# The emitter's price for a transpose on TensorE: one pass of the array in place of two, and the instruction order that follows

## The chip, the cores and the metric

The kernel runs on one core of one Trainium2 chip. The metric is the device time of one execution in microseconds (us). The profile is one execution seen by the hardware profiler; its span runs from the first to the last instruction. The engines are PE (TensorE, matmuls; PEld is its weight load), DVE (VectorE), ACT (ScalarE), POOL (GpSimd) and SP (the queue that issues every DMA). Each engine works through its own list of instructions in order, and an instruction that waits holds up all that stand behind it on that engine.

## The reference

Two layers over 2048 latent tokens of width 1024 with a context prefix of 256 tokens. Both layers are modulated by a conditioning vector ("ada"), normalised by RMS, gated by SiLU and added to the stream; a last RMSNorm ends the program.

```python
# layer 0 (even): windowed attention with context and sink, beside a bidirectional S5 state space
q, k, v, g_attn, u, g_ssm = jnp.split(a @ w_in, cuts, axis=-1)
o_attn = window_attention(q, k, v, kc, vc, sink) * jax.nn.silu(g_attn)
o_ssm, o_ssm_c = s5_branch(u, uc, ...)            # scans in both directions, GELU, GLU with a 512x512 matrix
y = jnp.concatenate([o_attn, o_ssm * jax.nn.silu(g_ssm)], axis=-1) @ w_out
# layer 1 (odd): pooling over 2, 4, 8 and 16 neighbours in four channel groups
u, gate = jnp.split(a @ w_in, 2, axis=-1)
p = jnp.einsum('btgc,gcd->btgd', multiscale_pool(u), pool_w) * pool_scale
y = (p * jax.nn.silu(gate)) @ w_out
```

Attention has 8 query heads on 2 key heads, blocks of 128 queries, each against three blocks of keys and the 256 context keys.

## The kernel before, in words

All data lie transposed (channels on the 128 partitions, tokens along the row). Large matrix products run in a 32-bit format of one pass, with operands split into a high and a low part: three matmuls of 128x128 by 512 columns make one product step (`products`, `mm`), eight steps a tile. Small products stay in plain f32.

**Who sets the order.** The kernel is written as some 35 generators, one for each stream of work (`t_main` for the input products, then the output product `t_out0` and the second layer; `t_ltab` and `t_lags` for the S5 lag kernels; `t_etab` for rotation tables; `t_gen`, `t_s5`, `t_rot`, `t_s5out` for the scan; `t_kv`, `t_qk`, `t_exp`, `t_norm`, `t_pv` for attention; `t_glu`, `t_fold`, `t_mix` beside it). While the program is built, an emitter (class `Threads`) keeps a clock for each engine. Every instruction is charged a duration (`use`, which calls `issue`): it starts at the latest of its engine's clock, its inputs and the readers of what it overwrites, and moves that clock. The stream that would be ready first by these clocks is continued next, and what it emits goes to the end of the engines' lists. The PE's charge passes through `array`, which doubles it while the emitter takes the array for slow. So a charge changes no instruction; it changes which stream comes next, and with it the place of instructions on all engines.

**What else looks at the clocks.** `lighter(n)` puts an elementwise operation on DVE or on POOL, whichever clock would be done first (with POOL's charge doubled); the splits, the rotation tables, the lag tables, the scan's rotations and others go through it. So a changed clock also moves operations between these two engines.

**Turns.** A turn is a 128x128 transpose: a matmul against the identity (`transpose`, line 508). There are 848: 624 in `t_pv`, 128 in `t_s5`, 48 in `t_kv` and 48 of two columns in the two ada streams.

**The stages, in the order of the span.** 0 to 50 us: modulation of layer 0. 50 to 260: norm, the `u` products, rotation and lag tables. 260 to 735: the other input products, with the S5 scan between them until 654. 735 to 1168: attention in 32 units (one key head and one block of 128 queries) and 156 items (one unit and one block of keys). For an item, `t_pv` issues four turns of probabilities into one of two PSUM banks, ACT copies the high part, DVE subtracts for the low part, and two matmuls follow; the turns of item j+1 stand ahead of the matmuls of item j. Beside it run `t_fold` (until 884 us) and `t_glu` (809 to 954 us); from 1032 us on the output product `t_out0` runs beside it. 1168 to the end: the rest of the output product and layer 1, matmul behind matmul.

`t_out0` needs the weight space that `t_glu` gives back at its end, and the mixed activations (`t_mixin`, `t_mix`) of a quarter of the tokens.

Of the kernel before, what the change touches and what calls it, by code (L numbers as in the profile page):

```python
# [289 lines left out]
def body(ctx: ExitStack, tc: tile.TileContext, I, out):  # L290
    nc = tc.nc
    V, G, S, TE = nc.vector, nc.gpsimd, nc.scalar, nc.tensor
# [166 lines left out]
    def use(e, c, outs, *ins, port=False):  # L459
        th.issue(ename[id(e)], c, outs, [x for x in ins if isinstance(x, bass.AP)], port)  # L460
# [43 lines left out]
        return TE.matmul(o, w, x, start=start, stop=stop)  # L504

    def transpose(o, i, ident):
        use(TE, 0.22, [o], i)
        return TE.transpose(o, i, ident)  # L508

    def dma(o, i):  # L510
# [66 lines left out]
    def t_ada0():  # L577
# [22 lines left out]
        for i in range(KT):  # L600
            g, half = divmod(i, 2)
            yield from arrived(w[i])
            t_ = shaped(w.pop(i), (4, 512))
            ps = bank(g % 2)[0:2]
            for k in range(4):
                mm(ps, s2.f[:, 4 * half + k], t_[:, k], i % 2 == k == 0, half == 1 and k == 3)
            yield
            load(i + NADA)
            if i == 1:
                flags.add("ada_l1")  # L610
            if half == 1:
                r = row.next()[0:2]
                act(r, ps, AF.Copy, scale=0.5)
                yield
                for j in range(4):
                    transpose(bank(2)[:, 8 * g + 2 * j:8 * g + 2 * j + 2], r[:, 128 * j:128 * (j + 1)], K["ident"][0:2, 0:2])
                yield
                sl = slice(2 * g, 2 * g + 2)
                for r, sh, gs in ((1, shc, gsc), (0, sh0, gs0)):
                    tt(V, sh[:, sl], got[:, 0, r, g], K["b0"][:, sl], OP.add)  # L620
                    tt(V, gs[:, sl], got[:, 1, r, g], K["b0"][:, 8:16][:, sl], OP.add)
                    stt(gs[:, sl], gs[:, sl], 1.0, K["g0"][:, sl], OP.add, OP.mult)
                flags.add(f"ada0{g}")
                yield
# [5 lines left out]
    def t_ada1():  # L630
# [13 lines left out]
        for blk in range(8):  # L644
            b = yield from get_bank()
            ps = bank(b)
            for i in range(4):
                yield from arrived(w[4 * blk + i])
                t_ = w.pop(4 * blk + i)
                for k in range(2):  # L650
                    mm(ps[0:2], silu.f[:, 2 * i + k], t_[:, k], i == k == 0, i == 3 and k == 1)
                yield
                load(4 * blk + i + NADA1)
            r = row.f[0:2]
            act(r, ps[0:2], AF.Copy, scale=0.5)
            yield
            for j in range(4):
                transpose(ps[:, 2 * j:2 * j + 2], r[:, 128 * j:128 * (j + 1)], K["ident"][0:2, 0:2])
            yield
            got = ps[:, 0:8:2]  # L660
            vec, sl = (gate0, sh1, gs1, gate1)[blk // 2], slice(4 * (blk % 2), 4 * (blk % 2) + 4)
            add = (K["b0"][:, 16:24], K["b1"][:, 0:8], K["b1"][:, 8:16], K["b1"][:, 16:24])[blk // 2]
            tt(V, vec[:, sl], got, add[:, sl], OP.add)
            put_bank(b)
            if blk // 2 == 2:
                stt(gs1[:, sl], gs1[:, sl], 1.0, K["g1"][:, sl], OP.add, OP.mult)
            if blk == 1:
                flags.add("gate0")
            yield
# [713 lines left out]
    def t_s5():  # L1383
# [6 lines left out]
        def trans(g, b):  # L1390
            ps = bank(b)
            o = s5.pop(g)
            for r in range(2):
                for kt in range(2):
                    i = 2 * r + kt
                    transpose(ps[:, 128 * i:128 * (i + 1)], o[:, r, 8 * kt:8 * kt + 8].rearrange("p j c -> p (j c)"),
                              K["ident"])
            return ps
# [1270 lines left out]
```

## Time and profile before

| | before |
|---|---|
| device time, three runs (us) | 1835.16, 1827.73, 1830.83; median 1830.83 |
| profiled execution: device time / span (us) | 1827.55 / 1825.8 |
| PE busy | 1717.7 us, 94% of the span |
| DVE / ACT / POOL busy | 1283.4 / 828.3 / 594.7 us |
| mean granted PE clock | 0.979 |
| instructions in the profile | 24990 |

A busy PE is not a PE at its peak: the ends of matmuls are modelled, and one matmul overlaps the next, so a start-to-start distance is the better price. A wait is put down to the event that came last. Where a table has "x4", four instructions are merged in one row that is named by the first of them.

### The profile page before, as it was taken

Reading aid. Unit: us, or ns where it says so; the run is one execution under the profiler, and the core shown is the slowest. Engines: PE = TensorE matmul, PEld = TensorE weight load, DVE = VectorE, ACT = ScalarE, POOL = GpSimd, SP = SyncE. Lnnn points to the kernel's source line nnn. Section 1 sums busy time; section 2 is a strip of 40 time slices with the busy share of each in tenths; the row PEclk is TensorE's granted clock in tenths of the full one; section 3 lists DMA queues with packets and bytes.
Section 4 is the critical chain, followed back from the end, with each engine's and each line's share of the span. In section 5 each row is a group of like instructions: output and inputs, shape, how many; then the busy total and the mean of one; then the engine's idle time right before and its main releaser. Section 6 shows DMA issues by size and latency. Waiting matters only on the chain.

```text
span 1825.8 us, 24990 instructions
## 1 busy us (share of the span) xinstructions
PE 1717.7 (94%) x8488; PEld 1366.8 (75%) x8488; DVE 1283.4 (70%) x2150; ACT 828.3 (45%) x1689; POOL 594.7 (33%) x722
## 2 busy tenths in 40 slices
PE   6899998979998999988897999999999999999997
PEld 1654465758887887777775788888888888888897
DVE  3569764997878945777888879687656764666634
ACT  4545431335444433687677766544322332222311
POOL 4887655663244410435363534230000000000000
PEclk9999998989998999999999999999999999999998
DMA  7777565235665456465855446687211263441332
GB/s 287 221 239 219 162 172 177 97 123 172 193 216 155 156 162 180 137 185 140 238 159 160 114 137 182 203 254 231 87 58 46 75 201 127 141 135 48 105 87 86
DMA packets 226000, 286.16 MB, mean 157 GB/s; under 512 B 60112, under 2 KB 155088, under 8 KB 224848
## 3 DMA queue, kind: packets, MB, share of 16 engines
q1 hardware_dynamic: 225872, 284.56, 51.6%
q8 instruction: 67, 1.10, 0.2%
q14 instruction: 61, 0.50, 0.1%
HBM read 204.60 MB, written 79.89 MB: 156 GB/s over the span
## 4 chain that ended last, share of the span: by engine, by line
PE 74%; DVE 9%; DMA 6%; ACT 4%; POOL 3%; issue 3%; SPq 1%; DVEq 0%; ACTq 0%; POOLq 0%
PE psum L504 71%; PE psum L508 3%; DVE x_r L464 2%; DVE core_f L464 2%; DVE x_f L464 2%; POOL core_f L464 2%; ACT x_f L498 2%; ACT x_r L498 1%; SPq L512 1%; POOL core_f L469 1%; DMA x_f<-u_scr 1%; DVE core_f L475 1%; DMA core_f<-a_scr 1%; DMA core_f<-sg_scr 1%; DMA core_f<-in_s5p 1%
## 5 line engine op out<-in xcount | busy, mean ns | idle before, releaser
L504 PE MATMUL psum<-x_r,core_r 128*128 128x512 f32 (+3 forms) x4536 | 1080.5, 393 | 5.7 <-ACT core_f L498 1.5
L504 PEld LDWEIGHTS psum<-x_r,core_r 128*128 128x128 f32 x4536 | 841.5, 189 | 199.1 <-issue 20.4
L504 PE MATMUL psum<-x_r 128*128 128x256 f32 (+3 forms) x1808 | 372.8, 348 | 13.7 <-DVE x_r L464 4.5
L464 DVE TENSOR_TENSOR core_f<-core_f 128x512 f32<-128x512 f32 (+20 forms) x443 | 301.3, 692 | 49.4 <-ACT core_f L498 22.0
L504 PEld LDWEIGHTS psum<-x_r 128*128 128x128 f32 x1808 | 284.0, 195 | 47.9 <-issue 12.9
L464 POOL TENSOR_TENSOR core_f<-core_f 128x32 f32<-128x32 f32 (+8 forms) x321 | 235.5, 748 | 178.9 <-ACT core_f L498 57.3
L464 DVE TENSOR_TENSOR core_r<-core_f,core_r 128x512 fp32r<-128x512 f32 (+1 forms) x182 | 135.1, 742 | 170.8 <-ACT core_r L498 168.1
L498 ACT ACTIVATE core_r<-core_f 128x512 fp32r<-128x512 f32 (+1 forms) x224 | 141.0, 632 | 220.6 <-PE psum L504 129.3
L498 ACT ACTIVATE core_f<-psum 128x512 f32<-128x512 f32 (+2 forms) x217 | 116.0, 535 | 257.9 <-PE psum L504 238.9
L498 ACT ACTIVATE x_r<-core_f 128x512 fp32r<-128x512 f32 (+5 forms) x173 | 127.0, 745 | 99.6 <-DVE core_f L475 69.0
L470 POOL TENSOR_SCALAR x_f<-x_f,core_f 128x640 f32<-128x640 f32 (+1 forms) x128 | 131.1, 1037 | 105.4 <-DVE core_f L492 66.7
L508 PE MATMUL psum<-core_f,x_f 128*128 128x128 f32 (+1 forms) x792 | 123.0, 279 | 30.5 <-DVE x_r L464 24.4
L464 DVE TENSOR_TENSOR x_r<-psum,x_r 128x512 fp32r<-128x512 f32 (+2 forms) x174 | 112.1, 649 | 48.9 <-ACT x_r L498 45.1
L508 PEld LDWEIGHTS psum<-core_f,x_f 128*128 128x128 f32 (+1 forms) x792 | 96.2, 144 | 62.8 <-DVE x_r L464 31.0
L498 ACT ACTIVATE x_f<-x_f,core_f 128x640 f32<-128x640 f32 (+2 forms) x155 | 123.5, 798 | 36.1 <-DVE core_f L475 32.4
L475 DVE SCALAR_TENSOR_TENSOR core_f<-core_f 128x512 f32<-128x512 f32 (+12 forms) x162 | 122.0, 762 | 20.8 <-DMA core_f<-h_scr 12.2
L498 ACT ACTIVATE core_f<-core_f 64x32 f32<-64x32 f32 (+7 forms) x224 | 83.4, 372 | 113.7 <-DVE core_f L475 94.9
L479 POOL COPY core_f<-core_f 128x16 f32<-128x16 f32 (+2 forms) x35 | 8.7, 262 | 369.1 <-DVE core_f L475 293.3
L464 POOL TENSOR_TENSOR core_r<-core_f,core_r 128x512 fp32r<-128x512 f32 x42 | 61.8, 1475 | 203.6 <-ACT core_r L498 203.6
L498 ACT ACTIVATE x_f<-psum 128x512 f32<-128x512 f32 (+5 forms) x187 | 77.7, 447 | 93.3 <-PE psum L504 80.7
L464 DVE TENSOR_TENSOR x_f<-x_f 128x512 f32<-128x512 f32 (+5 forms) x155 | 116.5, 780 | 3.4 <-ACT x_f L498 1.6
L498 ACT ACTIVATE x_r<-psum 128x512 fp32r<-128x512 f32 (+2 forms) x174 | 97.1, 562 | 48.1 <-PE psum L504 42.7
(64 smaller groups left out, 1314.0 us busy)
## 6 DMA issues: line engine op xcount, KB each, us to landing
core_f<-in_wo SPq DMA_DIRECT2D x48, 512.0 KB
core_f<-in_w SPq DMA_DIRECT2D x42, 512.0 KB
x_f<-in_adaM SPq DMA_DIRECT2D x32, 512.0 KB
core_f<-in_xT SPq DMA_DIRECT2D x45, 256.0 KB
x_f<-in_adaN SPq DMA_DIRECT2D x8, 1024.0 KB
o_scr<-core_f SPq DMA_DIRECT2D x32, 256.0 KB
x_f<-o_scr SPq DMA_DIRECT2D x16, 512.0 KB
sg_scr<-core_f SPq DMA_DIRECT2D x32, 256.0 KB
```

Of the source, the lines that this page charges most:

```text
L464: return e.tensor_tensor(o, a, b, op=op)
L469: return e.tensor_scalar(o, a, s1, None, op0=op0)
L470: return e.tensor_scalar(o, a, s1, s2, op0=op0, op1=op1)
L475: return V.scalar_tensor_tensor(o, a, s, b, op0=op0, op1=op1)
L479: return e.tensor_copy(o, a)
L498: return S.activation(o, i, f, **kw)
L504: return TE.matmul(o, w, x, start=start, stop=stop)
L508: return TE.transpose(o, i, ident)
L512: return nc.sync.dma_start(o, i)
```

## The change

One constant of the emitter. A turn of any size is charged 0.11 us on PE in place of 0.22 us (doubled, as before, while the emitter takes the array for slow). A plain f32 matmul of 128 columns keeps 0.22 us.

```diff
     def mm(o, w, x, start, stop):
         n = size(x)
         c = max(n, 256) / 2400.0 + 0.0135 if w.dtype == F32R else 2 * max(n / 1200.0 + 0.003, 0.11)
         use(TE, c, [o], w, x)
         return TE.matmul(o, w, x, start=start, stop=stop)

     def transpose(o, i, ident):
-        use(TE, 0.22, [o], i)
+        use(TE, 0.11, [o], i)
         return TE.transpose(o, i, ident)
```

The lists of PE, DVE, ACT, POOL and SP are the same up to the first turns and differ from there on. On PE they are the same again from the middle of the output product to the end. Of the 128 elementwise operations of the rotation tables, DVE had 64 and has 96; POOL had 64 and has 32. PE and ACT each have the same operations in number as before.

First place, PE, about 265 to 320 us of the trace: the lag products (48x272, two matmuls each, numbers 18 to 21 counted from 0) and the input products (128x512) between them. Before:

```order
L504 MATMUL psum<-core_f 48x272 x2
L504 MATMUL psum<-x_r,core_r 128x512 x24
L504 MATMUL psum<-core_f 48x272 x2
L504 MATMUL psum<-x_r,core_r 128x512 x54
L504 MATMUL psum<-core_f 48x272 x2
L504 MATMUL psum<-x_r,core_r 128x512 x30
```

Now:

```order
L504 MATMUL psum<-core_f 48x272 x2
L504 MATMUL psum<-x_r,core_r 128x512 x36
L504 MATMUL psum<-core_f 48x272 x2
L504 MATMUL psum<-x_r,core_r 128x512 x60
L504 MATMUL psum<-core_f 48x272 x2
L504 MATMUL psum<-x_r,core_r 128x512 x36
```

Lag products 19, 20 and 21 each stand behind more input products.

Second place, POOL, the same stretch: the end of the last rotation table (steps of 8x8, 8x16 and 8x32 elements, each four operations) and the lag table of product 20 (544 and 272 elements, two of each). Before:

```order
L464 TENSOR_TENSOR core_f<-core_f 128x8x8 x2
L464 TENSOR_TENSOR core_f<-core_f 128x256
L464 TENSOR_TENSOR core_f<-core_f 128x16x16
L464 TENSOR_TENSOR core_f<-core_f 128x8x16 x2
L464 TENSOR_TENSOR core_f<-core_f 128x512
L464 TENSOR_TENSOR core_f<-core_f 128x16x32
L464 TENSOR_TENSOR core_f<-core_f 128x8x32 x2
L464 TENSOR_TENSOR core_f<-core_f 128x544 x2
L464 TENSOR_TENSOR core_f<-core_f 128x272 x2
```

Now:

```order
L464 TENSOR_TENSOR core_f<-core_f 128x8x8 x2
L464 TENSOR_TENSOR core_f<-core_f 128x512
L464 TENSOR_TENSOR core_f<-core_f 128x256
L464 TENSOR_TENSOR core_f<-core_f 128x16x16
L464 TENSOR_TENSOR core_f<-core_f 128x8x16 x2
L464 TENSOR_TENSOR core_f<-core_f 128x544 x2
L464 TENSOR_TENSOR core_f<-core_f 128x272 x2
L464 TENSOR_TENSOR core_f<-core_f 128x544 x2
L464 TENSOR_TENSOR core_f<-core_f 128x272 x2
```

The step of 8x32 (four operations) has gone to DVE; the 128x512 row of the new list is the sum of a rotated key tile, which stood further down; the table of product 21 now follows whole on POOL.

Third place, PE, attention, where the last six matmuls of the GLU product (128x512 from x_r and core_r) stand. L508 with 128x128 is the turns of an item, x_r 128x512 x2 its two matmuls, and the 384 and 256 columns are scores of a later unit. Before:

```order
L508 MATMUL psum<-core_f,x_f 128x128 x4
L504 MATMUL psum<-x_r 128x512 x2
L504 MATMUL psum<-x_r 128x384 x2
L504 MATMUL psum<-x_r 128x256 x4
L504 MATMUL psum<-x_r 128x384 x2
L504 MATMUL psum<-x_r,core_r 128x512 x6
L508 MATMUL psum<-core_f,x_f 128x128 x4
L504 MATMUL psum<-x_r 128x512 x2
L508 MATMUL psum<-core_f,x_f 128x128 x4
L504 MATMUL psum<-x_r 128x512 x2
```

Now:

```order
L508 MATMUL psum<-core_f,x_f 128x128 x4
L504 MATMUL psum<-x_r 128x512 x2
L504 MATMUL psum<-x_r,core_r 128x512 x6
L508 MATMUL psum<-core_f,x_f 128x128 x4
L504 MATMUL psum<-x_r 128x512 x2
L508 MATMUL psum<-core_f,x_f 128x128 x4
L504 MATMUL psum<-x_r 128x512 x2
L504 MATMUL psum<-x_r 128x384 x2
L504 MATMUL psum<-x_r 128x256 x4
L504 MATMUL psum<-x_r 128x384 x2
```

Before, the turns of 70 items stand ahead of these last six, and the first six matmuls of the output product stand behind the turns of 106 items. Now it is 63 and 110. The items in between, with no large product beside them, are 36 before and 47 now.

## The prediction

> **What bounds the kernel now.** I read the page first, then a table by stage, then what PE waits for in the stages where it idles. On the page, the PE row of the 40 slices (45.6 us each; tenths busy, 9 is 90% or more):
>
> ```profile
> PE   6899998979998999988897999999999999999997
> PEclk9999998989998999999999999999999999999998
> ```
>
> PE is the bound nearly everywhere, and its work is the same before and after; so the time is PE's work plus its idle time. The stages, each with PE's busy time first, then PEld, DVE, ACT, POOL and the granted clock:
>
> ```profile
> 50.00:260.00 210.00, 200.56 (x800) 110.94 (x800) 150.14 (x232) 102.59 (x202) 152.41 (x261) 0.99 0.67 201
> 260.00:400.00 140.00, 118.05 (x515) 86.70 (x516) 103.61 (x139) 36.98 (x109) 90.39 (x93) 0.93 0.41 132
> 400.00:600.00 200.00, 191.13 (x1112) 166.66 (x1110) 164.39 (x254) 96.36 (x219) 78.97 (x61) 0.97 0.60 182
> 735.00:955.00 220.00, 197.40 (x1122) 167.10 (x1120) 177.30 (x341) 161.38 (x341) 104.91 (x86) 0.95 0.63 175
> 955.00:1032.00 77.00, 60.96 (x341) 47.89 (x340) 66.15 (x149) 59.50 (x138) 31.46 (x33) 0.93 0.45 122
> 1032.00:1168.00 136.00, 135.10 (x733) 114.18 (x732) 109.09 (x220) 88.27 (x185) 55.52 (x51) 1.00 0.58 172
> 1168.00:1826.00 658.00, 646.96 (x3087) 551.58 (x3085) 403.95 (x586) 206.31 (x341) 31.49 (x48) 0.99 0.40 123
> ```
>
> Idle on PE: 9.4 us at 50 to 260, 22.0 at 260 to 400, 8.9 at 400 to 600, 22.6 at 735 to 955, 16.0 at 955 to 1032, 0.9 beside the output product, 11.0 in the last 658 us. The last stage stands in the same order in both kernels. What can move is the idle time of the tables and the scan (22.0) and of attention without the output product (38.6).
>
> **The turn itself: 0.** No instruction changes. Whether the new price is the truer one, the trace tells:
>
> ```profile
> L508 PE MATMUL psum<-core_f,x_f x792: 195/273/477, 23.3 to 1168.2; 128*128 128x128 f32 x188, 2*128 2x2 f32 x10
> 1062.42 0.60 PE L508 MATMUL psum<-core_f,x_f 128*128 128x128 f32 x4
> 1062.77 0.71 PE L504 MATMUL psum<-x_r 128*128 128x512 f32 x2
> 384.36 2.05 PE L504 MATMUL psum<-x_f 128*128 128x128 f32 x16 [1.76 <-DVE core_f L464]
> 386.17 1.64 PE L504 MATMUL psum<-x_r,core_r 128*128 128x512 f32 x6
> ```
>
> Four turns take 0.35 us from the first start to the start of what follows, 0.09 each. Eight plain f32 matmuls of the same size are 16 records and take 1.81 us, 0.226 each. So 0.11 is near the truth for a turn, and 0.22 was right only for the plain matmul. Over 848 turns the emitter's PE clock ran 848 x 0.11 = 93 us ahead of this part of the work, two thirds of it in `t_pv` (69 us).
>
> The Trainium skill speaks against it: "TensorE: Matmul & The Clock Gate", Part 4, has a turn at about 275 ns in a kernel's context and says that it does not count as activity for the clock gate. Its 275 ns is this trace's record length (median 273 in the row above), not the distance between starts; at 275 the emitter should have charged more, and the sum of 848 would be an estimated 233 us in place of 76. The distance decides here, 0.09.
>
> **Tables, 50 to 260 us: 0, between 0 and +6.** 32 table operations go from POOL to DVE. By the forms, one costs DVE about 0.6 us on average (my estimate from mean durations of each form, 20 us in all), POOL loses about 17. DVE has 210 - 150 = 60 us free in this stage, so the cover is there. Without it, normalised rows come late and the `u` products wait; if three tenths of the 20 us lie open on a DVE that is then busy for 170 of 210 us, that is the +6. Below zero there is little: PE is already 96% busy.
>
> **Lag products 19 and 20, about 285 and 305 us: -5.4, between -8.4 and +3.5.**
>
> ```profile
> 285.04 1.09 PE L504 MATMUL psum<-core_f 128*48 128x272 f32 x4 [3.44 <-DVE core_f L464]
> 286.06 14.14 PE L504 MATMUL psum<-x_r,core_r 128*128 128x512 f32 x54
> 291.42 14.80 POOL L464 TENSOR_TENSOR core_f<-core_f 128x64 f32<-128x64 f32 x20 [9.37 <-DVE core_f L464]
> 300.28 6.49 DVE L464 TENSOR_TENSOR core_f<-core_f 128x1024 f32<-128x1024 f32 x4 [8.40 <-POOL core_f L464]
> 305.11 2.31 PE L504 MATMUL psum<-core_f 128*48 128x272 f32 x4 [4.91 <-POOL core_f L464]
> ...
> L464 POOL TENSOR_TENSOR core_f<-core_f 128x256 f32<-128x256 f32 x4 | 2.6, 679 | 0.2
> L464 POOL TENSOR_TENSOR core_f<-core_f 128x512 f32<-128x512 f32 x2 | 2.1, 1050 | 0.1
> ```
>
> Product 20 waits 4.91 us for its table, which POOL makes behind the last rotation table (the last two rows are POOL's groups at 290 to 306 us). The new order takes the step of 8x32 off POOL: two operations of 512 and two of 256, 2.1 + 1.36 = 3.5 us sooner. Six more input products stand ahead of product 20, 6 x 0.26 (14.14 over 54) = 1.6 us more cover. One rotation sum of 512 elements comes in ahead on POOL, 1.05 us. The wait falls to 4.91 - 3.5 - 1.6 + 1.05 = 0.9: -4.0. Product 19 gets 36 input products for 24 in front, 3.1 us of cover against a wait of 3.44, but its table now goes partly through POOL; I take less than half of it, -1.4. At best both waits go (3.44 + 4.91). At worst DVE, which takes the step over with evictions queued behind it, is as late as POOL gets early: +3.5.
>
> **From lag product 20 to the second output of the scan, 305 to 396 us: +3.5, between -6 and +7.6.**
>
> ```profile
> 305.00:396.00 91.00, 77.28 (x349) 55.90 (x349) 82.37 (x109) 26.81 (x80) 62.42 (x55) 0.93 0.32 106
> 373.61 2.02 PE L504 MATMUL psum<-core_f 128*48 128x272 f32 x4 [6.87 <-DVE x_f L475]
> 395.85 2.50 PE L504 MATMUL psum<-x_f 128*128 128x128 f32 x10 [4.96 <-DVE core_f L464]
> ```
>
> DVE is busy 82 of 91 us with POOL at 62, and PE's two long waits end on DVE: this stretch goes at the pace of these two. I counted what stands between the same two products in both orders, each operation at its form's typical duration: DVE 59.5 us before and 64.4 now, POOL 53.4 and 57.9, PE 67.7 and 71.8. By the sum of DVE and POOL the stretch grows by 122.3/112.9, 8.3% of 91 = 7.6 us, of which 4.1 are PE work that is then done: +3.5. If the waits of 6.87 and 4.96 fall half away in the new arrangement, -6; if the PE work brought in gives nothing back later, +7.6.
>
> **Attention until the output product starts: +2.6, between -8 and +10.** The GLU's last matmuls stand behind 63 items in place of 70, the output product's first behind 110 in place of 106. So 47 items in place of 36 run with no large product beside them. PE idles 16.0/36 = 0.45 us per such item, and 22.6/70 = 0.32 per item with GLU or fold beside it: 11 x 0.45 - 7 x 0.32 = 4.9 - 2.3 = +2.6 (four items fewer beside the output product are worth 4 x 0.9/50, nothing). The waits are mostly the turns' own:
>
> ```profile
> PE psum L508 <- DVE x_r L464: 23.5, 23, 3.1
> ```
>
> Turns wait for DVE to have read the bank (23.5 us between 735 and 1032). DVE is busy 66 of 77 us at 955 to 1032, with preparations for the output product that now spread over more items: half of the 16.0 could go (-8). The upper end is the stretch's own worst piece, under the rivals.
>
> **Sum.** 0 + 0 - 5.4 + 3.5 + 2.6 = +0.7 on the profiled execution's 1827.55 us, 1828 us. That execution lies 3.3 us under the median of the three runs, 1830.83, whose spread is 7.4; I stay at 1828. The ends of the terms do not fall together; their roots of squares give -14 and +14 about it, 1814 to 1842 for this forecast alone.
>
> **Rival 1: the truer clock pays everywhere (faster).** With 93 us of work taken off the emitter's PE clock that the chip never did, what it believes ready is nearer to what is ready, so stalls shrink on all engines. For it: the two waits above shrink just where the order changed. Against it: the other charges (DMA, POOL, ACT) are as they were, and the long waits at 373 and 396 us end on DVE, not on PE. A quarter of the idle 22.0 + 38.6 us is 15: 1827.55 - 15 = 1813.
>
> **Rival 2: the cover is spent early (slower).** The turns of a bare item wait for DVE, and 47 in a row pay what the worst piece of 36 pays now:
>
> ```profile
> 960.42 0.63 PE L508 MATMUL psum<-core_f,x_f 128*128 128x128 f32 x4 [2.26 <-DVE x_r L464]
> 962.27 1.11 PE L508 MATMUL psum<-core_f,x_f 128*128 128x128 f32 x4 [0.76 <-DVE x_r L464]
> 967.86 0.66 PE L508 MATMUL psum<-core_f,x_f 128*128 128x128 f32 x4 [0.84 <-DVE x_r L464]
> 971.74 0.63 PE L508 MATMUL psum<-core_f,x_f 128*128 128x128 f32 x4 [0.66 <-DVE core_f L464]
> 973.67 0.66 PE L508 MATMUL psum<-core_f,x_f 128*128 128x128 f32 x4 [0.83 <-DVE x_r L464]
> ```
>
> These are 5.35 us in the eight items from 960 to 976, 0.67 per item; 47 x 0.67 = 31.5 against 16.0 now: +15.5, 1843 us. It decides once the bare stretch is longer by more than DVE can fill with the output product's preparation. Against it: DVE's list holds no more work than before, only elsewhere, and the 955 to 1032 mean is 0.45, not 0.67.
>
> **Rival 3: bare turns let the clock fall (slower).** The granted clock is 0.93 at 955 to 1032 and 1.00 beside the output product. If the array ran all 11 added items at half speed, each would take its 60.96/36 = 1.7 us of PE work twice: +18.6, 1846 us. The skill's rule that turns do not hold the clock up (same page and part) would bring this; at 0.93 the trace shows a seventh of that stretch slow, and at 1.00 beside turns with the output product none.
>
> That the change moves nothing is out, since the lists differ; that it moves nothing which PE waits for lies within the forecast (1827.6).
>
> **Chances.** Forecast 0.40, rival 1 0.32, rival 2 0.22, rival 3 0.06. A measurement of this kernel tells about 0.5% from no change, 9 us: below 1821.7 is faster, above 1840 slower. Of the forecast's share a tenth falls on either side, of rival 1's four fifths are faster, of rival 2's three fifths slower, of rival 3's most. Faster 0.04 + 0.26 = 0.30, slower 0.04 + 0.13 + 0.06 = 0.23, same 0.47. The range has to reach both rivals' centres: 1806 to 1848.
>
> **What would show it.** Right: PE's waits at lag products 19 and 20 under 3 us together in place of 8.4; PE idle between lag product 20 and the second output of the scan not more than 4 us larger; the bare stretch about 100 us long with PE idle 18 to 24; the same PE busy time within 5 us; turns still 0.09 apart. The forecast is wrong if idle time in the bare stretch passes 30 us (rival 2), if its clock falls under 0.8 (rival 3), or if PE idles under 45 us from 260 to the start of the output product (rival 1).

## The result, and the profile after

The changed kernel takes 1812.05 us (median of 4 runs, 1810.34 to 1814.35) against 1830.67 (4 runs, 1827.73 to 1835.16) of the kernel before beside it: ratio 0.9894, 95% interval 0.9875 to 0.9913. It is faster by 1.06%. The forecast was 1828; the number that came is that of rival 1, 1813. In the runs further down, one execution of the kernel with all turns at 0.30 took 7997.18 us against 1852 to 1858 of its other three, and is left out. The profiled span went from 1825.8 to 1810.0 us, and that difference, 15.8 us, is what the traces can be asked about.

PE in the 40 slices of the changed kernel's page, tenths busy, and the granted clock below it:

```profile
PE   6899999979989998899888999999999999999997
PEclk9999999989999999999999999999999999999999
```

The seventh slice (271 to 317 us; 274 to 319 before) was 8 on PE and 8 on its clock and is 9 on both. The first row of each page, busy time of the whole execution (before, and after):

```profile
PE 1717.7 (94%) x8488; PEld 1366.8 (75%) x8488; DVE 1283.4 (70%) x2150; ACT 828.3 (45%) x1689; POOL 594.7 (33%) x722
```

```profile
PE 1713.7 (95%) x8488; PEld 1358.0 (75%) x8488; DVE 1290.5 (71%) x2168; ACT 828.2 (46%) x1689; POOL 597.9 (33%) x704
```

The same 8488 matmuls: PE idles 96.3 us in place of 108.1 (span less busy time), -11.8, and is busy 4.0 us less for the same work. The 4.0 are a question of the clock, as the next rows show.

**Where the time went.** I took the time between two products that both lists have, less the PE work that stands between them in each list (each matmul at its usual spacing). What is left is idle time and slow time together, "lost" below:

| stretch | before, us lost | after | difference |
|---|---|---|---|
| start to lag product 18 | 44.9 | 45.7 | +0.8 |
| lag product 18 to the start of lag product 20 | 10.6 | 0.5 | -10.1 |
| there to the second scan output | 23.2 | 20.3 | -2.9 |
| there to the first product of attention | 29.0 | 28.8 | -0.2 |
| attention until the output product starts | 80.3 | 77.0 | -3.3 |
| from there to the end | 12.3 | 12.1 | -0.2 |

So four fifths of the gain lie in about 30 us around 300 us. Windows over this place, columns as in the prediction (PE, PEld, DVE, ACT, POOL busy, granted clock, DMA share, GB/s), first before, then after:

```profile
286.00:300.00 14.00, 14.00 (x55) 11.21 (x54) 1.38 (x6) 2.59 (x7) 8.04 (x16) 0.88 0.36 117
300.00:318.00 18.00, 13.07 (x44) 8.47 (x44) 12.38 (x13) 2.46 (x7) 13.34 (x12) 0.81 0.33 113
318.00:400.00 82.00, 68.41 (x326) 51.05 (x325) 78.55 (x104) 26.00 (x76) 55.65 (x46) 0.94 0.28 93
```

```profile
286.00:300.00 14.00, 14.00 (x61) 10.84 (x60) 9.29 (x12) 1.39 (x3) 13.21 (x19) 1.00 0.81 267
300.00:318.00 18.00, 18.00 (x77) 12.98 (x76) 17.63 (x23) 4.26 (x14) 12.32 (x12) 1.00 0.37 127
318.00:400.00 82.00, 70.72 (x342) 51.71 (x341) 75.47 (x105) 31.70 (x84) 49.15 (x40) 0.94 0.30 100
```

Two things are to be seen. PE's idle time at 300 to 318 us is gone and the clock of 0.88 and 0.81 is 1.00. And DVE, which did 1.38 us of work in 14 before, does 9.29, and 17.63 of 18 after that. In the stretch behind it is nearly full in both (78.55 and 75.47 of 82).

The timeline of PE after, at the rows that the prediction showed of before (285.04, 286.06, 305.11):

```profile
286.34 1.12 PE L504 MATMUL psum<-core_f 128*48 128x272 f32 x4
287.39 13.94 PE L504 MATMUL psum<-x_r,core_r 128*128 128x512 f32 x60
301.25 1.12 PE L504 MATMUL psum<-core_f 128*48 128x272 f32 x4
302.30 8.50 PE L504 MATMUL psum<-x_r,core_r 128*128 128x512 f32 x36
310.73 1.12 PE L504 MATMUL psum<-core_f 128*48 128x272 f32 x4
```

Lag products 19, 20 and 21 wait for nothing. Sixty input products take 13.94 us, 0.232 each; before, 54 took 14.14, 0.262 each. The windows of 2 us of the kernel before tell why:

```profile
284.00:286.00 2.00, 0.96 (x4) 0.41 (x4) 1.81 (x4) 0.00 (x0) 0.00 (x0) 1.00 0.89 290
286.00:288.00 2.00, 2.00 (x6) 1.60 (x6) 0.00 (x0) 0.00 (x0) 0.00 (x0) 0.60 0.63 222
288.00:290.00 2.00, 2.00 (x6) 1.54 (x5) 0.00 (x0) 0.00 (x0) 0.00 (x0) 0.54 0.51 173
290.00:292.00 2.00, 2.00 (x10) 1.62 (x9) 1.38 (x6) 1.53 (x4) 0.58 (x2) 1.00 0.91 264
304.00:306.00 2.00, 0.89 (x2) 0.23 (x2) 1.97 (x3) 0.00 (x0) 2.00 (x2) 0.50 0.00 0
308.00:310.00 2.00, 2.00 (x6) 1.59 (x5) 1.96 (x4) 0.00 (x0) 1.92 (x4) 0.50 0.57 178
312.00:314.00 2.00, 2.00 (x10) 1.66 (x9) 0.35 (x1) 0.00 (x0) 1.50 (x1) 1.00 0.00 0
```

Behind the wait of 3.44 us (it ended at 285.04) the clock is 0.60 and 0.54 for 4 us, with 6 matmuls in 2 us in place of 10; around the wait of 4.91 (ended 305.11) it is 0.50 from 304 to 310. By the spacings that is 54 x 0.030 = 1.6 us for the first, and for the second 2.31 - 1.12 = 1.2 for lag product 20 itself and 8.47 - 30 x 0.236 = 1.4 for the 30 input products: 4.2 us. With the two waits, 8.35 + 4.2 = 12.6 us, which is the -10.1 and -2.6 of the -2.9 in the table. Behind that, the scan gives nothing more and takes nothing back.

The Trainium skill ("TensorE: Matmul & The Clock Gate", Part 1) has the array fall to half rate after an idle window of about 3.4 us and come back after a busy one as long. These rows agree in the main: idle 3.44, then about 4 us near half; idle 4.91, then about 5, both somewhat longer than one such window.

**What started sooner.** VectorE's rows where the last rotation table's second step (the one of 128x32) stands, before and then after. It follows the small operation (L475) on the output of a lag product:

```profile
290.43 0.22 DVE L475 SCALAR_TENSOR_TENSOR x_f<-core_f,psum 16x16 f32<-16x16 f32 x1 [4.58 <-ACT core_f L498]
290.68 0.59 DVE L464 TENSOR_TENSOR core_f<-core_f 128x32 f32<-128x32 f32 x4
```

```profile
282.15 0.23 DVE L475 SCALAR_TENSOR_TENSOR x_f<-core_f,psum 16x16 f32<-16x16 f32 x1
282.40 1.15 DVE L464 TENSOR_TENSOR core_f<-core_f 128x32 f32<-128x32 f32 x4
294.22 4.96 DVE L464 TENSOR_TENSOR core_f<-core_f 128x512 f32<-128x512 f32 x4
```

And the row of GpSimd after that answers the 291.42 one of before, the steps behind it:

```profile
285.02 7.22 POOL L464 TENSOR_TENSOR core_f<-core_f 128x272 f32<-128x272 f32 x14 [1.92 <-DVE core_f L464]
```

Before, the step stands on VectorE behind the output of lag product 19, which itself waits 3.44 us; GpSimd idles 9.37 us for it, and then VectorE 8.40 us for GpSimd. Now it stands behind the output of lag product 18, 8.3 us sooner, and GpSimd idles 1.92. The turns are as they were, 0.35 us from the first start to the start of the next product:

```profile
1041.65 0.60 PE L508 MATMUL psum<-core_f,x_f 128*128 128x128 f32 x4
1042.00 0.71 PE L504 MATMUL psum<-x_r 128*128 128x512 f32 x2
```

The prediction read 0.09 us a turn out of such a pair of rows, and that is too low. The four records end 0.60 us after the first one starts and are 0.27 us long each (the prediction's median of 273 ns), so the last starts 0.33 us behind the first: 0.11 us from turn to turn. The product behind starts only about 0.03 us after the last turn, and its two matmuls then start 0.31 us apart (0.71 less a record of 0.40) where one input product takes 0.23, so that nothing is gained there. The price of the change, 0.11, is the distance that the trace has.

Attention, from its first turns to the last product of the GLU and from there to the output product, after:

```profile
721.00:924.00 203.00, 183.35 (x1049) 154.88 (x1048) 165.40 (x307) 148.56 (x312) 101.84 (x79) 0.97 0.65 183
924.00:1021.00 97.00, 79.51 (x456) 61.68 (x455) 85.78 (x190) 72.54 (x167) 45.06 (x44) 0.95 0.45 122
```

PE idles 19.7 us beside 63 items and 17.5 us over the 47 bare ones (22.6 and 16.0 before, the prediction's rows).

### The profile page after: what moved, and what is told of

Its sections match the earlier page's. It is cut to its first block, busy times and chain, and to the rows that moved or that the text cites. A ratio compares the mean times of both kernels' runs of the same rounds, so it can differ in the third digit from the quotient of the medians.

```text
span 1810.0 us, 24987 instructions
## 1 busy us (share of the span) xinstructions
PE 1713.7 (95%) x8488; PEld 1358.0 (75%) x8488; DVE 1290.5 (71%) x2168; ACT 828.2 (46%) x1689; POOL 597.9 (33%) x704
## 4 chain that ended last, share of the span: by engine, by line
PE 56%; DVE 4%; DMA 3%; ACT 2%; issue 1%; POOL 1%; SPq 1%; DVEq 0%; ACTq 0%; POOLq 0%
PE psum L504 53%; PE psum L508 3%; DVE x_r L464 1%; ACT x_r L498 1%; DMA core_f<-sg_scr 1%; ACT x_f L498 1%; DMA wu_scr<-core_f 1%; SPq L512 1%; POOL x_f L470 1%; DVE core_f L464 1%; DMA core_f<-k_scr 1%; DVE core_f L475 1%; DVE x_f L483 1%; DVE x_f L464 0%; ACT core_f L498 0%
## 5 line engine op out<-in xcount | busy, mean ns | idle before, releaser
L464 DVE TENSOR_TENSOR core_f<-core_f 128x512 f32<-128x512 f32 (+21 forms) x474 | 315.6, 679 | 46.4 <-ACT core_f L498 19.1
L464 DVE TENSOR_TENSOR core_r<-core_f,core_r 128x512 fp32r<-128x512 f32 (+1 forms) x185 | 139.3, 753 | 184.4 <-ACT core_r L498 181.5
L464 POOL TENSOR_TENSOR core_f<-core_f 128x32 f32<-128x32 f32 (+8 forms) x288 | 213.7, 754 | 117.4 <-DVE core_f L464 33.1
L498 ACT ACTIVATE core_f<-psum 128x512 f32<-128x512 f32 (+2 forms) x221 | 120.1, 546 | 267.2 <-PE psum L504 244.4
L508 PE MATMUL psum<-core_f,x_f 128*128 128x128 f32 (+1 forms) x792 | 122.0, 275 | 27.8 <-DVE x_r L464 18.9
L464 DVE TENSOR_TENSOR x_r<-psum,x_r 128x512 fp32r<-128x512 f32 (+2 forms) x174 | 112.2, 649 | 48.4 <-ACT x_r L498 46.4
L508 PEld LDWEIGHTS psum<-core_f,x_f 128*128 128x128 f32 (+1 forms) x792 | 94.8, 142 | 62.4 <-DVE x_r L464 27.4
L498 ACT ACTIVATE core_f<-core_f 64x32 f32<-64x32 f32 (+8 forms) x221 | 81.1, 368 | 122.2 <-DVE core_f L475 95.6
L475 DVE SCALAR_TENSOR_TENSOR core_f<-core_f 128x512 f32<-128x512 f32 (+13 forms) x162 | 125.0, 782 | 15.7 <-ACT core_f L498 8.3
L464 POOL TENSOR_TENSOR core_r<-core_f,core_r 128x512 fp32r<-128x512 f32 x39 | 55.4, 1421 | 243.8 <-ACT core_r L498 243.1
L464 DVE TENSOR_TENSOR x_r<-core_f,x_r 128x512 fp32r<-128x512 f32 (+5 forms) x93 | 88.1, 956 | 34.4 <-ACT x_r L498 33.9
L498 ACT ACTIVATE x_f<-psum 128x512 f32<-128x512 f32 (+5 forms) x183 | 73.0, 432 | 81.9 <-PE psum L504 76.7
```

What stands on the lines that cost most here:

```text
L464: return e.tensor_tensor(o, a, b, op=op)
L475: return V.scalar_tensor_tensor(o, a, s, b, op0=op0, op1=op1)
L498: return S.activation(o, i, f, **kw)
```

## The experiments

Three theories. **Truer price** (rival 1): the less the emitter's charge departs from the chip's, the fewer stalls, so the gain goes with the charge taken off. **Place**: the gain is what went at lag products 19 to 21, by the early start of the last rotation table, with the waits and slow windows that hung on it. **Lottery**: a new price deals a new order everywhere, and what it brings is not tied to the price. All times are medians; a ratio is against the kernel before on the same chip, whose median was 1830.2 to 1832.3 us in these runs.

### Parts of the change

The turns ahead of attention alone: those of both tables of modulations (L616 and L658, the second shown) and those of the scan's outputs (L1397). `c` is the charge of a turn, 0.22 where none is given:

```diff
-    def transpose(o, i, ident):
-        use(TE, 0.22, [o], i)
+    def transpose(o, i, ident, c=0.22):
+        use(TE, c, [o], i)
...
-                transpose(ps[:, 2 * j:2 * j + 2], r[:, 128 * j:128 * (j + 1)], K["ident"][0:2, 0:2])
+                transpose(ps[:, 2 * j:2 * j + 2], r[:, 128 * j:128 * (j + 1)], K["ident"][0:2, 0:2], 0.11)
...
-                              K["ident"])
+                              K["ident"], 0.11)
```

> The price of 0.11 is given to the turns ahead of the scan alone (the two tables of modulations and the 16 turns ahead of the second scan output), 0.22 stays for the turns of kv and pv in attention (74 of the 93 us of charge). The list is that of the change up to attention. Place theory (the gain is the waits and the half-clock windows at lag products 19 to 21 that vanished, -12.5 us, and attention brought -3.4): about -12 us, ratio 0.993; the three input-product stretches at 286 to 318 us at clock 1.00. Truer-price theory (gain in proportion to the charge that is taken off, 19 of 93 us here): -4 us or less, ratio 0.998. Lottery theory (any new list gives its own number): no number, but the tables and the scan here are those of the change, so -12 as well up to 400 us and anything between -10 and +10 behind it.

Measured 1821.09 us, ratio 0.9942 (0.9919 to 0.9965).

The turns of attention alone:

```diff
-                transpose(ps[:, 64 * j:64 * (j + 1)], v[:, 128 * j:128 * (j + 1)], K["ident"][0:64, 0:64])
+                transpose(ps[:, 64 * j:64 * (j + 1)], v[:, 128 * j:128 * (j + 1)], K["ident"][0:64, 0:64], 0.11)
...
-                transpose(tp[:, 128 * h:128 * (h + 1)], pss[u][h][:, c:c + 128], K["ident"])
+                transpose(tp[:, 128 * h:128 * (h + 1)], pss[u][h][:, c:c + 128], K["ident"], 0.11)
```

> 0.11 for the turns of kv and pv in attention alone, 0.22 for all turns ahead of it. The list is that of the kernel before up to attention, and then 52 bare items in place of 36 (47 in the change). Place theory: the waits of 3.4 and 4.9 us at lag products 19 and 20 stay, and the total moves by -3 to 0 us, ratio 0.998 to 1.000. Truer-price theory: four fifths of the charge are here, so about -15 us, ratio 0.992. My forecast's step for attention (0.45 us per bare item, 0.32 per covered one): 16 more bare items, +5 to +7 us.

Measured 1834.09 us, ratio 1.0009 (0.9997 to 1.0021): +2 us, between the -3 to 0 of the place theory and the +5 to +7 of the forecast's step.

The modulations' 48 small turns alone (the first diff without its last place):

> 0.11 for the 48 small turns of the modulations alone (2x128 to 128x2, ahead of 60 us), 5 us of charge. The lags stand as in the change: 24, 24, 36, 60, 36 input products ahead of lag products 17 to 21. Place theory: about -12 us by lag product 21, and in all -12 give or take 4. Truer-price theory: a twentieth of the charge, -1 us. Either way the stretch up to 260 us stays as it is.

Measured 1805.82 us, ratio 0.9868 (0.9840 to 0.9896).

The windows at 300 to 318 us of attention alone, and of the modulations alone:

```profile
300.00:318.00 18.00, 13.94 (x48) 9.71 (x47) 11.85 (x12) 1.26 (x3) 15.76 (x15) 0.81 0.18 65
```

```profile
300.00:318.00 18.00, 18.00 (x77) 13.09 (x76) 17.64 (x22) 4.26 (x14) 13.45 (x12) 1.00 0.38 127
```

The price in proportion to the charge falls here: four fifths of the charge bring nothing (+2 us), 5 us of it bring 26. The waits and the 0.81 stay in the one and go in the other, as the place theory says. What it does not say is the size: the early part alone was expected at -12 and is at -11, but the modulations alone, expected at -12 give or take 4, are at -26. The table further down shows where those two part: behind the second scan output, up to attention (29.6 against 20.5 us lost), and in attention.

### The place

The kernel before in its own order, the four operations of the step of 8x32 of the last rotation table executed by VectorE (the first is shown); `tt` executes on `on` and charges `e`, so the emitter is told nothing:

```diff
+                on = V if (part, k) == (3, 5) else None
-                tt(e, y, old, s_, OP.mult)
+                tt(e, y, old, s_, OP.mult, on)
...
```

> The list of the kernel before, only the four operations of the last rotation table's step of 8x32 are executed by VectorE in place of GpSimd (the emitter is told nothing). My prediction's term: lag product 20 waits 3.5 us less (4.9 to 1.4), if VectorE is not late by as much. Place theory with the clock: where the wait falls under about 1.5 us the slow stretch behind it (0.81 at 300 to 318 us) goes too, so -3.5 and about -3 more, -6 us in all by lag product 21. If VectorE is late by what GpSimd gains: 0 to +3. Truer-price theory: 0, since no price changes.

Measured 1829.21 us, ratio 0.9995 (0.9978 to 1.0012). The lost time falls by 4.3 us by lag product 21, where -6 was expected, and by lag product 26 it is given back (-0.4). Its VectorE:

```profile
297.21 9.60 DVE L464 TENSOR_TENSOR core_f<-core_f 128x512 f32<-128x512 f32 x8 [4.75 <-POOL core_f L464]
```

It ends this at 306.81 us; before, its four operations from 300.28 ended at 306.77. PE's wait of 4.91 us is 0.65, but VectorE, which in the kernel before is busy 78.55 of the next 82 us, is no sooner through, and PE waits for it later. My prediction had priced this step at -3.5 us and never asked where it would be given back.

Then the second step itself, four operations of 32 elements, from VectorE to GpSimd, again in the order of before (the same edit with `(part, k) == (3, 1)` and `G`):

> The list of the kernel before, only the four operations of the last rotation table's second step (2x8x2 = 32 elements) are executed by GpSimd in place of VectorE, where they stand behind the output of lag product 19 (290.4 us) and hold up the table (GpSimd idle 9.4 us, then VectorE 8.4 us). New place theory (the table's start sets VectorE's work, and VectorE is the bound of the next 80 us): the table starts about 8 us sooner; the wait of 4.9 at lag product 20 goes, the clock at 286 to 318 is near 1.00, VectorE idles some 8 us less at 260 to 318 and the gain stays up to the first product of attention: -6 to -10 us in all, ratio 0.9945 to 0.9965. Cover theory (the gain comes from 60 and 36 input products in place of 54 and 30 ahead of the lag products): as in the run with the step of 8x32 on VectorE, -4 by lag product 21 and given back by lag product 26: 0 in all. Truer-price theory: 0.

Measured 1825.30 us, ratio 0.9976 (0.9956 to 0.9996). Its VectorE (this execution stood 2.8 us later than before at lag product 18), and under it the row of before that answers the last one:

```profile
293.98 0.22 DVE L475 SCALAR_TENSOR_TENSOR x_f<-core_f,psum 16x16 f32<-16x16 f32 x1 [4.96 <-ACT core_f L498]
...
296.88 6.54 DVE L464 TENSOR_TENSOR core_f<-core_f 128x1024 f32<-128x1024 f32 x4 [1.33 <-POOL core_f L464]
...
316.00 0.69 DVE L464 TENSOR_TENSOR core_f<-core_f 128x512 f32<-128x512 f32 x1 [7.00 <-DMA e_scr<-core_f]
```

```profile
317.47 0.69 DVE L464 TENSOR_TENSOR core_f<-core_f 128x512 f32<-128x512 f32 x1 [5.12 <-DMA e_scr<-core_f]
```

VectorE waits 1.33 us for the table in place of 8.40, and the lost time falls by 7.3 us from lag product 18 to 21. Then the next wait in line takes a part: VectorE needs the table back from memory, 7.00 us in place of 5.12. What is left, 4.3 us, is there at the second scan output; the median says 4.9 for the whole. The local mechanism holds; the expected -6 to -10 was too much by that second wait.

The other way round, the change with its table held back:

```diff
+                if (part, k) == (3, 2):
+                    for _ in range(8):
+                        G.tensor_tensor(x_(2, NE, 32), E[:, :, :, 0:32], E[:, :, :, 0:32], op=OP.mult)
                 tt(e, y, old, s_, OP.mult)
```

> The changed kernel, with eight idle products of 512 elements on GpSimd (about 1.05 us each, 8.4 us, into the table's scratch, which the next step overwrites) ahead of the last rotation table's third step: the list stays, the table comes about as late as before. New place theory: 6 to 12 us of the gain go again, 1818 to 1824, with waits at lag products 20 and 21 and half-clock slices back. Cover theory: 0 to +3, 1812 to 1815.

Measured 1820.49 us, ratio 0.9948 (0.9932 to 0.9965), 8.4 us above the changed kernel. VectorE, and PE, at the rows that answer 294.22 and 301.25 of the change:

```profile
299.83 4.89 DVE L464 TENSOR_TENSOR core_f<-core_f 128x512 f32<-128x512 f32 x4 [8.11 <-POOL core_f L464]
```

```profile
303.59 0.66 PE L504 MATMUL psum<-core_f 128*48 128x272 f32 x2 [3.97 <-POOL core_f L464]
```

The 8.11 us on VectorE and a wait at lag product 20 are back in spite of the 60 input products in front, so it is the table's start and not the cover that counts. This is the strongest of the runs: one cause added to the list of the change takes 8.4 of its 18.6 us. It also keeps GpSimd busy for 9.5 us more, which this run alone cannot part from the late table; the run before it, which adds no work, points the same way with 4.9 us. The other 10 are not this: by the table below, 3.5 lie ahead of the second scan output and 3.9 in attention, the latter within the 4 us by which executions differ there.

### Other prices

All turns at 0.09, 0.165, 0.05 and 0.30 (one number in the line of the change each):

> Every turn priced at 0.09, what the trace has between the starts of two turns, in place of the change's 0.11. Truer-price theory: as the change or a little better, 1806 to 1812. Place theory (the gain hangs on what stands at lag products 19 to 21; it is lost where GpSimd makes the last rotation table's step of 8x32 straight ahead of the lag table, as before, and here it does): nothing of the 12.5 us, 1822 to 1834. Lottery theory: anything between 1800 and 1840; the sign against the change is even odds.

> Every turn priced at 0.165, halfway between 0.22 and 0.11. Truer-price theory: halfway, about 1821. Place theory: 24, 54 and 12 input products ahead of lag products 19, 20 and 21 (before 24, 54, 30; change 36, 60, 36) and the step of 8x32 on GpSimd ahead of the lag table, so the two waits stay and a third is likely: 1830 to 1840. Lottery theory: anything between 1800 and 1840.

> Every turn priced at 0.05, too cheap by as much (0.04) as 0.11 is over the 0.09 of the trace, doubled. Truer-price theory: a little worse than the change, 1812 to 1818. Place theory: the step of 8x32 is off GpSimd here too, but 18 and 24 input products ahead of lag products 20 and 21 in place of 60 and 36: half of the gain there, 1818 to 1828. Lottery theory: anything between 1800 and 1840.

> Every turn priced at 0.30, further off than the 0.22 before: 68 us more on the emitter's clock. Truer-price theory: slower than before by about as much as 0.11 was faster at the ratio of the charges (0.08 to 0.11), +13, 1844. Place theory: POOL has all small steps of the last rotation table, 42, 24 and 24 input products ahead of lag products 19 to 21: 1825 to 1840. Lottery theory: anything between 1800 and 1840, faster than before with a chance of four in ten.

Measured in this order: 1825.09, 1829.36, 1844.45 and 1852.82 us. The expectations took 0.09 for the distance between turns; it is 0.11 (above), so the change itself has the truest of these prices and 0.09 is 0.02 too low. 0.165 is no different from before.

No theory fits all four. The truer-price theory as put down missed at 0.165 (1821 expected) and at 0.05 (1812 to 1818), and had the sign at 0.30 (1844). The place theory had 0.09 and, within 1 us, 0.165, but not for its reason: both lists lose 8 to 12 us less up to the second scan output, where it expected nothing to go (table below), and lose most of it again behind. At 0.05 and 0.30 it missed (1818 to 1828, 1825 to 1840), and so did the lottery theory, whose 1800 to 1840 was too narrow.

A price that was right made wrong by the same sum at the same place, the turns left at 0.22; `less` is 0.055 in the two calls of the modulations, L606 and L651:

```diff
-    def mm(o, w, x, start, stop):
+    def mm(o, w, x, start, stop, less=0.0):
...
-        use(TE, c, [o], w, x)
+        use(TE, c - less, [o], w, x)
...
```

> The turns keep 0.22; the 96 large matmuls of the modulations are charged 0.055 less each (0.859 to 0.804, where the trace has 0.86 between starts): the same 5.28 us off the emitter's clock at the same place as in the run with the modulations' turns alone at 0.11, but from a price that was right. Truer-price theory: no gain, 0 to +5 us. Lottery theory: the order at lag products 17 to 21 is new again (24, 12, 60, 12 input products ahead of 17 to 20, the whole last rotation table between 18 and 19); the table is one lag earlier than before and so -5 to -10 by the second scan output, and attention deals anything between -5 and +20 on top; sign open.

Measured 1825.91 us, ratio 0.9978 (0.9959 to 0.9997): -4 us, where the truer-price theory had 0 to +5.

And a run that was meant to price the modulations' turns alone at 0.30:

> The modulations' 48 turns alone at 0.30 (further from the truth by 0.08 each, 3.8 us of charge), all others at 0.22. Truer-price theory: +3 us or less, 1831 to 1834. Lottery theory: the whole list is another from there on; the last rotation table is done before lag product 16 here, so the stretch at 286 to 318 us should run without the two waits; with what attention deals, anything between 1805 and 1850.

Measured 1889.80 us, ratio 1.0323 (1.0288 to 1.0359), beyond what any of the theories had put down. But its edit does more than its expectation says:

```diff
-        c = max(n, 256) / 2400.0 + 0.0135 if w.dtype == F32R else 2 * max(n / 1200.0 + 0.003, 0.11)
+        c = max(n, 256) / 2400.0 + 0.0135 if w.dtype == F32R else 2 * max(n / 1200.0 + 0.003, 0.30)
```

Every plain f32 matmul of fewer than 356 columns is charged 0.60 us, too, where one of 128 columns had 0.22. The trace has 552 such matmuls; by this formula they put about 191 us more on the emitter's clock, against 3.8 for the 48 turns. So the run says what a price made wrong on many small matmuls costs, and nothing of the 48 turns by themselves.

All runs that change a price, and the three of the place, with the time lost by stretch from the trace (to the second scan output from lag product 18; to attention; in attention until the output product):

| kernel | median us | ratio (95%) | to lag 18 | to scan output | to attention | in attention |
|---|---|---|---|---|---|---|
| before, 0.22 | 1830.7 | 1 | 44.9 | 33.8 | 29.0 | 80.3 |
| the change, 0.11 | 1812.1 | 0.9894 (0.9875 to 0.9913) | 45.7 | 20.8 | 28.8 | 77.0 |
| all 0.05 | 1844.5 | 1.0058 (1.0038 to 1.0078) | 52.4 | 19.1 | 44.2 | 87.6 |
| all 0.09 | 1825.1 | 0.9967 (0.9956 to 0.9977) | 44.9 | 25.5 | 31.5 | 86.2 |
| all 0.165 | 1829.4 | 0.9993 (0.9979 to 1.0008) | 44.6 | 21.9 | 33.8 | 90.3 |
| all 0.30 | 1852.8 | 1.0125 (1.0102 to 1.0148) | 57.8 | 19.0 | 42.6 | 96.4 |
| early turns 0.11 | 1821.1 | 0.9942 (0.9919 to 0.9965) | 46.2 | 20.5 | 29.6 | 81.3 |
| attention's turns 0.11 | 1834.1 | 1.0009 (0.9997 to 1.0021) | 48.2 | 32.4 | 30.9 | 87.4 |
| modulations' turns 0.11 | 1805.8 | 0.9868 (0.9840 to 0.9896) | 45.5 | 19.1 | 20.5 | 77.2 |
| plain f32 matmuls 0.60, modulations' turns 0.30 | 1889.8 | 1.0323 (1.0288 to 1.0359) | 62 | 9 | 85 | 93 |
| false price, same sum | 1825.9 | 0.9978 (0.9959 to 0.9997) | 45.6 | 31.1 | 31.3 | 79.1 |
| before, 8x32 on VectorE | 1829.2 | 0.9995 (0.9978 to 1.0012) | 45.2 | 32.2 | 27.6 | 84.2 |
| before, second step on GpSimd | 1825.3 | 0.9976 (0.9956 to 0.9996) | 47.7 | 29.5 | 26.4 | 83.5 |
| the change, table held | 1820.5 | 0.9948 (0.9932 to 0.9965) | 44.0 | 30.3 | 30.9 | 76.4 |

The two rows in which only four operations changed engines in the order of before have 84.2 and 83.5 in the last column, against 80.3: about 4 us of that column is the difference between executions and says nothing.

What follows. A shift of 5 us at one and the same place gives -26 us from one price (modulations at 0.11) and -4 from another (false price). Prices brought nearer to the trace do not add up: 672 turns of attention give +2, the 48 of the modulations -26, and those 48 with the 128 of the scan -11. Attention with its turns at 0.11 loses 77.0 in one order and 87.4 in another, and at 0.22, with only turns or modulations priced otherwise, between 77.2 and 84.2. And two edits that tell the emitter nothing move the time by 4.9 and 8.4 us. So the gain does not go with the charge taken off, and the truer-price theory in the form of rival 1 has fallen.

A weak form, that a price further from the truth deals worse orders on average, stays open, and these runs speak for it more than against it. Of the six prices given to all turns, the true one, 0.11, is the fastest; 0.09, 0.165, 0.22 and 0.30 follow in the order of their distance from it, though 0.165 and 0.22 cannot be told apart. Only 0.05 stands out of line: 0.06 off, and slower than 0.22, 0.11 off. The wrong price on 552 plain matmuls gave the slowest of all. Six prices are too few to part that from chance; several close to 0.11 would have helped, and were not run.

The place theory has to be put more sharply, and the false price shows how. I had expected -5 to -10 there by the second scan output, since the table stands one lag product earlier; it is -2.7. Its rows on GpSimd, VectorE and PE:

```profile
286.08 14.79 POOL L464 TENSOR_TENSOR core_f<-core_f 128x64 f32<-128x64 f32 x20 [9.47 <-DVE core_f L464]
294.93 6.49 DVE L464 TENSOR_TENSOR core_f<-core_f 128x1024 f32<-128x1024 f32 x4 [8.39 <-POOL core_f L464]
299.76 2.31 PE L504 MATMUL psum<-core_f 128*48 128x272 f32 x4 [5.31 <-POOL core_f L464]
```

These are the three waits of before (9.37, 8.40, 4.91), one lag product earlier. Not the number of the lag product counts, but the pattern: the second step on VectorE behind the output of a lag product, and all the rest of the table between this product and the next. The lists with this pattern (before, attention's turns, the false price, the kernel before with 8x32 on VectorE), the one with the second step on GpSimd, which has half of it, and the one with the table held have 29.5 to 33.8 in the column to the scan output; the other lists have 9 to 25.5, though 0.05 and 0.30 lose 7 and 13 us more ahead of lag product 18. This grouping was made after the runs, and a wait alone does not decide it: PE waits 5.67 us for GpSimd at lag product 20 with 0.165 and 4.91 us at lag product 19 with 0.05, and the columns there are 21.9 and 19.1.

The modulations' turns alone, 1805.8 us, is the fastest of all, and faster than before; that it beats the change is not shown, since the two intervals overlap. Why it gains 26 us where the place accounts for about 15 is open: it loses 8.5 us less than the kernel before between the second scan output and attention, and no run asks why.

## Why the prediction was wrong where it was

By its own steps; the differences are those of the table of lost time. The time lies in the stated range of 1806 to 1848, but the range reached that far only for rival 1's sake: the forecast's own band, 1814 to 1842, begins above it, no change that can be told had the largest chance (0.47), and faster had 0.30. That the number is rival 1's is luck, as its reason has fallen.

- **The turn itself, 0.** Right that it does not change; the 0.09 was a misreading, turns start 0.11 us apart before and after, and 848 of them would be 93 us and not 76. The 69 us of `t_pv` are three quarters of the 93 us of charge, not two thirds. **Tables, 0:** right, +0.8.
- **Lag products 19 and 20, -5.4, bounds -8.4 to +3.5.** Right in place and sign, and the step that failed: -10.1 up to the start of product 20, and -2.6 more directly behind it. It fell short on three counts. The lower bound held the two waits and nothing else; the half-clock windows behind them cost 4.2 us, which windows of the trace before would have shown. I had quoted the granted clock of 0.93 for the stage and made it a rival for attention only. Next, I gave product 19 less than half of its wait because its table goes partly through GpSimd; the wait went altogether. And I followed the table from the back (which engine has the step of 8x32) where the front mattered: its second step of 0.59 us, a lag product earlier on VectorE.
- **From lag product 20 to the second scan output, +3.5.** Wrong, and for a reason that the run with 8x32 on VectorE shows. The pace of DVE and POOL, 8.3% more work between two products, was taken over the whole stretch from the start of product 20. But VectorE came into it with work done ahead, 26.9 us at 286 to 318 in place of 13.8. The time from the one product to the other grew by 1.2 us (90.7 to 91.9) with 4.1 us more PE work in it. The term was to be costed from VectorE's idle time at 260 to 400, not from a point on PE: 36.4 us before and 20.8 now, 15.6 less, against 13.0 us gained from lag product 18 to the second scan output.
- **Attention, +2.6.** The other sign, within its bounds: -3.3, no more than the 4 us by which executions differ there. The 0.45 us per bare item became 17.5/47 = 0.37, the 0.32 per covered item 19.7/63 = 0.31. A mean per item is no price of an item: lists with 42 to 52 bare items lose 76.4 to 96.4 us in attention, those with 36 lose 79.1 to 84.2.
- **Rival 1** gave the number, and for a wrong reason: -15 was a quarter of the idle time, and the price alone pays nowhere in proportion. **Rival 2** (cover spent early): the bare stretch is 96 us with PE idle 17.5, a little under the 18 to 24 of the forecast and far from 31.5. **Rival 3** (bare turns let the clock fall): 0.95 there against 0.93 before; no.
- **Signs to look for.** Waits at 19 and 20 under 3 us: 0. PE idle from product 20 to the second scan output at most +4: 13.7 before, 92.00 - 80.90 = 11.1 now. PE busy within 5 us: -4.0. The sign for rival 1, PE idle under 45 us from 260 to the start of the output product, did not come: it went from 72.3 (260 to 1032) to 62.0 (260 to 1021). In the stages that the sum was made of it fell from 60.6 to 48.4 (11.3 at 260 to 400, 19.7 and 17.5 in attention).

The two windows of the changed kernel that these points use beside the ones above:

```profile
260.00:400.00 140.00, 128.72 (x587) 94.80 (x586) 119.25 (x165) 45.05 (x123) 85.55 (x85) 0.96 0.47 152
301.00:393.00 92.00, 80.90 (x368) 58.39 (x366) 86.30 (x113) 30.99 (x88) 60.55 (x50) 0.94 0.31 102
```

The two from 260 us to the start of the output product, before and after:

```profile
260.00:1032.00 772.00, 699.73 (x3768) 579.93 (x3769) 599.04 (x1048) 408.48 (x921) 330.78 (x292) 0.96 0.55 162
260.00:1021.00 761.00, 698.98 (x3806) 575.29 (x3805) 612.96 (x1064) 410.87 (x926) 335.08 (x289) 0.97 0.56 167
```

## What to carry to other kernels

Ask of a wait that vanishes whether the engine that is the bound of the next stretch gets through any sooner: the step of 8x32 took 4.3 us off PE's wait and brought nothing, the second step took 7.3 off and kept 4.3. Price an idle gap of 3 to 5 us on TensorE with the slow time behind it, here 4.2 us on top of 8.35. And where a planner sets the order, the gain of a corrected price is not in proportion to the charge corrected: here one part of it brought 26 us and the largest part nothing. Time several, and ask of the one that wins which waits its order took away.

## What the hardware showed that was not expected

More idle time came with more busy time for the same work. The same 8488 matmuls kept PE busy for these times in the fastest and in the slowest of the profiled executions (modulations' turns alone at 0.11, and plain f32 matmuls at 0.60):

```profile
PE 1707.6 (95%) x8488; PEld 1355.2 (75%) x8488; DVE 1287.7 (71%) x2171; ACT 827.8 (46%) x1689; POOL 599.1 (33%) x701
```

```profile
PE 1737.6 (92%) x8488; PEld 1377.7 (73%) x8488; DVE 1280.8 (68%) x2186; ACT 826.9 (44%) x1689; POOL 547.7 (29%) x686
```

With spans of 1801.5 and 1889.0 us PE idles 93.9 and 151.4: 57.5 us more idle time, and 30.0 more busy time for the same work, 0.52 us per microsecond. The mean granted clock is 0.986 in the one and 0.967 in the other. Not every wait has this price: before, the product that waited 1.76 us at 384.36 ran at full pace (the prediction's rows). The Trainium skill ("TensorE: Matmul & The Clock Gate", "Why this matters for your kernels") advises against idle gaps of more than about 3 us between bursts of matmuls; the gap of 3.44 us, after which the clock was down for 4 us, agrees.
